# A decoder trunk on one core: hand-set spacing of the scan's chunks, earlier sums for the gated norm, and a new order of the projected rows

## The chip, the cores and the metric

The kernel runs on one core of a Trainium2 chip. It uses that core's matrix engine (PE, with its weight loads shown as PEld), the vector engine (DVE), the scalar engine (ACT), GpSimd (POOL) and the sync engine (SP), which here only issues transfers. The metric is the device time of one execution in microseconds. Three runs of the kernel before gave 2872.22, 2872.91 and 2874.28 us; their median is 2872.91 us. The profile is a separate execution.

## The reference, cut to what matters

The program is a two-layer trunk over 1040 tokens (16 learned ones and 1024 given) of width 1024. Layer one is a Mamba-2 style mixer and a gated convolutional feed-forward part, layer two is stick-breaking attention and another feed-forward part. The change touches only the mixer and the first lines behind it. Cut to its core, the mixer computes:

```python
z, xbc, dt_raw = jnp.split(u @ w_in, [2048, 2048 + 3072], axis=-1)
xbc = silu(causal_conv4(xbc, conv_w, conv_b))
xs, b_in, c_in = jnp.split(xbc, [2048, 2048 + 512], axis=-1)
# per group g of 4 (8 heads of 64 channels each), chunk by chunk:
y_diag = einsum('bgcls,bgecls,bcsgep->bclgep', cb, decay_in, xdt)
y = y_diag + y_off(state) + xs * d_skip
hg = (y * silu(z)).reshape(b, L, 4, 512)
hg = hg * rsqrt(mean(hg * hg, axis=-1) + eps) * gate_g
out = hg @ w_out
```

The chunk length is free, since any split of the scan gives the same sum; the kernel uses nine chunks of 116 tokens.

## The kernel before, in words

All matrices are float32 split into a high and a low part, so each product is three matmuls (`mm3`, L164 to L166). Rows of the program are 128 channels by 1040 tokens. A row is made in three **projection tiles** of 348, 348 and 344 tokens; one tile is 24 matmuls into one PSUM bank. Tiles of token block 2 go to the bank `ex`, those of blocks 0 and 1 to the two banks `mm`.

There are two kinds of projection tile. An **in-tile** makes a third of a row of x, b or c: after the matmuls, ACT writes the first tap of the convolution (L288), DVE adds three taps (L292), and ACT applies silu when the next tile settles (L480). A **gate tile** makes a third of a row of z: ACT takes silu out of PSUM (L512), DVE multiplies it onto the scanned row (`product`, L519), and with the next tile ACT squares the product (L524) and DVE adds it to the sum of squares (L528, L530).

`mixer` first loads and transposes the tokens with tiles from a pool named `start`, makes the six rows of group 0 in an order that the planner sets (`stream(into(0))`), and then enters a part whose order on PE, DVE, ACT and POOL is that of the program text (`manual_schedule`). SP is not in that list, and instructions of later parts may still be placed in between by the planner. In this part the scan of the four groups runs, nine chunks each. Around each chunk stand `ssd_front` (the products of b and c, transposes, weighting by the decays) and `ssd_back` (the new state, the outputs, the skip). Between the two, the program pulls projection tiles from the generator `work = stream(blocks)`. I number these tiles from 0 to 101: into(1) is 0 to 17, gate(0) 18 to 29, into(2) 30 to 47, gate(1) 48 to 59, into(3) 60 to 77, gate(2) 78 to 89, gate(3) 90 to 101. Two of them come before the first chunk. The chunks of groups 0 and 3 then take about two each, those of groups 1 and 2 take 4, 3, 3, 4, 3, 3, 4, 3, 3, and the last six come behind the last chunk. With the first of a chunk's tiles the loads of the next chunk's decays (`ssd_decays`, tiles D and E) are issued, with the second ACT computes them (L614, L615), with the third DVE multiplies c onto them (L618).

When a group's gate tiles are done, `gate_norm` normalises each token block: a matmul with ones sums the squares over partitions (L542), ACT copies that out of PSUM (L543), loads a function table (L188), takes logarithm and exponential (L546, L547), and DVE refines the root in four steps (`refine`, L551 to L553). Before, these calls are keyed so that block j runs ahead of tile n = 31 + j, 61 + j and 91 + j. For groups 0 and 1 the refinement and then four `spill` steps are queued in `self.spread`, of which one is taken after each tile; a spill scales one x row in three instructions (L557) and POOL stores it to memory (L706). For group 2 refinement and scaling follow at once, but for block 2 the scaling, which is spread. Group 2's rows stay in place, and `out_proj` splits them into high and low parts (`split`, L174 and L175) outside the ordered part. Group 3's norm is done by `end`.

All long rows come from one pool of 28 buffers (`Q`): 16 hold the normalised input u, six a group's rows. A row of group g + 2 can be written only when a buffer of group g is free, thus after its store has ended. Decays, states and the chunk's other tiles come from a pool named `ssd`, opened after `start` has been closed.

```python
calls[3 * len(todo) + 1 + j] = lambda f=f, j=j: f(j)
for _ in range((tiles * (c + 1) + 8) // 9 - given):
self.spread += [lambda q=q: spill(q) for q in range(4)]
dk = pool.tile([P, 1024], F32, tag="D", name=self.nm("D"))
```

Of the kernel before, what the change touches and what calls it, by code (L numbers as in the profile page):

```python
# [8 lines left out]
F32 = mybir.dt.float32  # L9
# [4 lines left out]
P = 128  # L14
D = 1024
# [28 lines left out]
DT0 = 0  # L44
LAG = 2
EARLY = 2

NW = 8
SUMS = ((6, 1), (3, 6), (7, 6), (3, 5), (5, 7)), ((4, 7), (2, 1))
# [19 lines left out]
class Trunk:  # L69
# [411 lines left out]

        return self.a["w_in"][col // P], tile

    def in_group(self, u, g, out):


        def block(col, cv):
# [13 lines left out]

    def gate_group(self, u, g, x, acc, later):

# [29 lines left out]

        return [block(q) for q in range(4)]

    def gate_norm(self, g, x, acc, j, table=True):
        s0, n = TT[j]
        nc, width = self.nc, DI // GROUPS
        tt = nc.vector.tensor_tensor
        v, r = acc.pop(j)[:, :n], self.tmp("y")[:, :n]  # L540
        ps = (self.mm if j else self.ex)("ms")[:, :n]
        nc.tensor.matmul(ps, self.ones, v, start=True, stop=True)  # L542
        nc.scalar.activation(v, ps, AF.Copy)  # L543
        if table:
            self.ln_exp()
        nc.scalar.activation(r, v, AF.Ln, scale=1.0 / width)  # L546
        nc.scalar.activation(r, r, AF.Exp, scale=-0.5)  # L547

        def refine():
            for _ in range(2):  # L550
                tt(v, v, r, op=ALU.mult)  # L551
            nc.vector.tensor_scalar(v, v, -0.5 / width, 1.5, op0=ALU.mult, op1=ALU.add)
            tt(r, r, v, op=ALU.mult)  # L553

        def scale(q):
            xq = x[q][:, s0 : s0 + n]
            nc.vector.scalar_tensor_tensor(xq, xq, self.par("gate_norm", 4 * g + q), r, op0=ALU.mult, op1=ALU.mult)  # L557

        return refine, scale

    def settle(self):

# [4 lines left out]
    def stream(self, blocks, w0=None):  # L567


        calls = {}  # L570
        todo = []
        for src, f in blocks:
            if src is None:
                for j in range(3):
                    calls[3 * len(todo) + 1 + j] = lambda f=f, j=j: f(j)
            else:
                todo.append((src, f))
        w = [w0 or self.load_w(todo[0][0], D)]
        for n in range(3 * len(todo)):
            i, j = divmod(n, 3)  # L580
            if j == 0:
                if i + 1 < len(todo):
                    w.append(self.load_w(todo[i + 1][0], D))
                cur = w.pop(0)
            if n in calls:
                calls.pop(n)()
            todo[i][1](cur, j)
            if self.spread:
                self.spread.pop(0)()
            yield  # L590
        self.settle()
        for f in chain(self.spread, calls.values()):
            f()

    def ssd_decays(self, g, ct, c, pool):

        nc = self.nc
        h0 = GH * g
        t0, n = CH[c]
        cc = 3 * (c % 3) + c // 3  # L600
        dk = pool.tile([P, 1024], F32, tag="D", name=self.nm("D"))
        dk = dk[:n, : GH * CB].rearrange("p (h l) -> p h l", h=GH)
        nc.sync.dma_start(dk, self.acs_d[c, h0 : h0 + GH].unsqueeze(0).to_broadcast([n, GH, CB]))
        dk = dk[:, :, :n]
        ce = None
        if c:
            ce = pool.tile([P, GH * CB], F32, tag="E", name=self.nm("E"), bufs=2)
            ce = ce.rearrange("p (h l) -> p h l", h=GH)
            nc.sync.dma_start(ce, self.ea_d[c, h0 : h0 + GH].unsqueeze(0).to_broadcast([P, GH, CB]))
            ce = ce[:, :, :n]  # L610
        yield dk, ce

        for i in range(GH):
            nc.scalar.activation(dk[:, i], dk[:, i], AF.Relu, scale=-1.0, bias=self.cols[:n, 1, cc, h0 + i : h0 + i + 1])  # L614
        nc.scalar.activation(dk, dk, AF.Exp, scale=-1.0)  # L615
        yield
        if c:
            nc.vector.tensor_tensor(ce, ce, ct[:, t0 : t0 + n].unsqueeze(1).to_broadcast([P, GH, n]), op=ALU.mult)  # L618
        yield
# [60 lines left out]
    def mixer(self, mx):  # L680
# [4 lines left out]
            dt = self.dt_path(*dt, mx)  # L685
        with self.tc.tile_pool(name="ssd", bufs=3) as pool:
            nc = self.nc
            yd, rows = [None] * 4, [[] for _ in range(4)]
            accs = [{} for _ in range(4)]
            done, waiting = [], []  # L690

# [4 lines left out]
                    waiting.append((j, f))  # L696

            def gate(g):
                scales = []

                def spill(q):
                    if q == 0:
                        yd[g] = self.dp.tile([4, P, L], F32, tag=f"y{g}_d", name=f"y{g}_d")
                    for f in scales:
                        f(q)
                    nc.gpsimd.dma_start(yd[g][q], rows[g][q][:, :L])  # L706

                def norm(j):
                    refine, scale = self.gate_norm(g, rows[g], accs[g], j)
# [17 lines left out]
            into = lambda g: self.in_group(u, g, rows[g])  # L727
# [8 lines left out]
            with self.tc.manual_schedule(engines={E.PE, E.DVE, E.Activation, E.Pool}):  # L736
# [3 lines left out]
                    next(work)  # L740
                for g in range(GROUPS):
                    *x, bt, ct = rows[g]
                    tiles, given = (18 - EARLY, 30, 30, 18)[g], 0
                    state = None
                    for c in range(9):
                        for _ in ahead:
                            pass
                        ops = self.ssd_front(g, x, bt, ct, c, dk, pool)
                        now = dk, ce
                        for _ in range((tiles * (c + 1) + 8) // 9 - given):  # L750
                            next(work)
                            if given == (tiles * c + 8) // 9:
                                nxt = (g, ct, c + 1) if c < 8 else (g + 1, rows[g + 1][5], 0) if g < 3 else None
                                ahead = self.ssd_decays(*nxt, pool) if nxt else iter([(None, None)])
                                dk, ce = next(ahead)
                            else:
                                next(ahead, None)
                            given += 1
                        state = self.ssd_back(g, x, c, *now, *ops, state, pool)
                        if g == 3:  # L760
                            done.append(c)
                            todo, waiting[:] = waiting[:], []
                            for w in todo:
                                later(*w)
                for _ in work:
                    pass

        def end():
            for j in range(3):
                refine, scale = self.gate_norm(3, rows[3], accs[3], j, j == 0)  # L770
                refine()
                for q in range(4):
                    scale(q)

        return hd, [r[:4] for r in rows], yd, end

    def out_proj(self, hd, ys, yd, end, pool):

        a = self.a
        h = [None] * KD  # L780
        banks = cycle((self.mm, self.lg, self.ex, self.mm, self.lg))
        for i, g in enumerate((2, 0, 1)):
            ops = [self.split(ys[g][q] if yd[g] is None else self.fetch(yd[g][q], "y"), "y") for q in range(4)]
            for f in range(KD):
                w = self.load_w(a["w_out_f"][g, f], 4 * P)
                if i == 0:
# [7 lines left out]
        ops = [[self.split_half(ys[3][q][:, L // 2 * x : L // 2 * (x + 1)], "y") for q in range(4)] for x in range(2)]  # L794
# [814 lines left out]
    def run(self, ctx):  # L1609
        tc = self.tc  # L1610
        with self.banks() as self.lp:
            with tc.tile_pool(name="mx", bufs=1) as mx:
                hd, ys, yd, end = self.mixer(mx)
            self.rp = ctx.enter_context(tc.tile_pool(name="rp", bufs=1))
            with tc.tile_pool(name="ff0", bufs=2) as pool:
                d, *forms = self.out_proj(hd, ys, yd, end, pool)
# [79 lines left out]
```

## Time and profile before

| what | value |
|---|---|
| median of three runs | 2872.91 us |
| profiled execution, time | 2871.28 us |
| profiled execution, span | 2869.6 us |
| mean granted PE clock | 0.995 |
| PE, DVE, ACT, POOL busy | 98%, 70%, 54%, 22% |
| chain that ended last | PE 81%, DVE 6%, ACT 4% |
| loading, transposing and rows of group 0 | about 0 to 123 us |
| scan with projection tiles 0 to 101 | 123.5 to 658 us |

Times in the views are microseconds from the start of the span. A group of instructions is named by its source line, its engine, its operation and its output and input tiles. Busy PE time counts pipelined matmuls from issue to a modelled end, so a matmul of 0.32 us may follow the one before it after 0.16 us.

### The profile page before, as it was taken

The page shows a single profiled execution, that of the slowest core. Times are in us where ns is not written, and L with a number is a line of the kernel's source. Part 1 is how long each engine was busy: PE and PEld are TensorE (multiplying, and loading weights), DVE is VectorE, ACT ScalarE, POOL GpSimd, SP SyncE. Part 2 cuts the span into 40 slices and gives each one's busy share as a digit, 9 for nine tenths or more (in the row PEclk, how much of TensorE's full clock was granted, in tenths as well). Part 3 has the DMA queues.
Part 4 walks back from the last instruction along what each step waited for, and adds up shares of the span by engine and source line. Part 5 has one row for each costly group of instructions (what it writes and reads, how often), then busy time and mean ns, then how long its engine had stood idle before and what let it go on. Part 6 is the DMA issues. An engine that isn't in the chain of part 4 may idle for free.

```text
span 2869.6 us, 54962 instructions
## 1 busy us (share of the span) xinstructions
PE 2815.9 (98%) x21808; PEld 2705.5 (94%) x21808; DVE 2003.3 (70%) x3736; ACT 1559.2 (54%) x3067; POOL 619.1 (22%) x542
## 2 busy tenths in 40 slices
PE   8999999999999999999999999999998999999998
PEld 5999898989999999999999999999998999999888
DVE  5685858776578656558886666666679565657895
ACT  5576767773245555556334555555636555555442
POOL 0000000000004666660000111101102666661000
PEclk9999999999999999999999999999999999999999
DMA  6233333324221222226232222222441222225331
GB/s 170 75 111 93 118 87 114 105 60 160 84 98 64 78 79 78 80 84 208 67 132 87 62 68 67 63 69 57 143 148 54 82 80 78 80 82 184 110 110 60
DMA packets 134128, 274.69 MB, mean 96 GB/s; under 512 B 16464, under 2 KB 68304, under 8 KB 133872
## 3 DMA queue, kind: packets, MB, share of 16 engines
q1 hardware_dynamic: 128560, 260.26, 28.4%
q10 hardware_dynamic: 4048, 6.36, 0.6%
q0 software_dynamic: 1264, 4.57, 0.4%
q8 instruction: 171, 2.80, 0.4%
q14 instruction: 85, 0.70, 0.1%
HBM read 203.02 MB, written 53.21 MB: 89 GB/s over the span
## 4 chain that ended last, share of the span: by engine, by line
PE 81%; DVE 6%; ACT 4%; issue 1%; DMA 0%; ACTq 0%; DVEq 0%; SPq 0%
PE p L166 10%; PE p L165 10%; PE p L164 10%; PE acc L166 8%; PE acc L165 8%; PE acc L164 8%; PE pj L164 5%; PE pj L165 5%; PE pj L166 5%; PE lg L1400 3%; PE po L1437 3%; PE wT L1422 3%; ACT D L614 1%; DVE xbc L292 1%; DVE bl L917 1%
## 5 line engine op out<-in xcount | busy, mean ns | idle before, releaser
L164 PE MATMUL pj<-uh,wh 128*128 128x348 f32 (+2 forms) x1536 | 502.2, 327 | 7.2 <-DVE xbc L292 6.1
L165 PE MATMUL pj<-ul,wh 128*128 128x348 f32 (+2 forms) x1536 | 495.6, 323 | 0.0
L166 PE MATMUL pj<-uh,wl 128*128 128x348 f32 (+2 forms) x1536 | 492.4, 321 | 0.0
L164 PE MATMUL p<-bh,fh 128*128 128x262 f32 (+1 forms) x1408 | 400.2, 285 | 9.0 <-DVE p L1041 5.2
L165 PE MATMUL p<-bl,fh 128*128 128x262 f32 (+1 forms) x1408 | 401.1, 285 | 0.4
L166 PE MATMUL p<-bh,fl 128*128 128x262 f32 (+1 forms) x1408 | 400.0, 284 | 0.0
L165 PE MATMUL p<-bl,wh 128*128 128x262 f32 (+1 forms) x1056 | 301.5, 286 | 1.9 <-DVE bl L917 1.9
L164 PE MATMUL p<-bh,wh 128*128 128x262 f32 (+1 forms) x1056 | 301.8, 286 | 1.5 <-ACT bh L916 1.0
L166 PE MATMUL p<-bh,wl 128*128 128x262 f32 (+1 forms) x1056 | 302.5, 286 | 0.0
L164 PEld LDWEIGHTS pj<-uh,wh 128*128 128x128 f32 x1536 | 289.2, 188 | 10.4 <-issue 7.7
L165 PEld LDWEIGHTS pj<-ul,wh 128*128 128x128 f32 x1536 | 289.6, 189 | 1.8 <-issue 0.6
L166 PEld LDWEIGHTS pj<-uh,wl 128*128 128x128 f32 x1536 | 289.1, 188 | 0.0
L164 PEld LDWEIGHTS p<-bh,fh 128*128 128x128 f32 x1408 | 268.1, 191 | 10.3 <-DVE p L1041 5.6
L292 DVE SCALAR_TENSOR_TENSOR c<-p,params,c 128x260 f32<-128x260 f32 (+1 forms) x440 | 207.8, 481 | 90.9 <-ACT c L288 89.0
L165 PEld LDWEIGHTS p<-bl,fh 128*128 128x128 f32 x1408 | 267.3, 190 | 1.4 <-DVE bl L917 1.2
L166 PEld LDWEIGHTS p<-bh,fl 128*128 128x128 f32 x1408 | 267.4, 190 | 0.2
L972 POOL TENSOR_TENSOR fl<-x,fh 128x1024 fp32r<-128x1024 f32 x80 | 192.5, 2406 | 256.0 <-ACT fh L971 255.9
L1041 DVE TENSOR_TENSOR p<-p,ft 128x262 f32<-128x262 f32 (+1 forms) x176 | 76.5, 436 | 214.2 <-ACT ft L1038 125.2
L165 PE MATMUL acc<-gl,wh 128*128 128x260 f32 (+1 forms) x672 | 211.1, 319 | 0.6 <-DVE gl L1139 0.5
L166 PE MATMUL acc<-gh,wl 128*128 128x260 f32 (+1 forms) x672 | 208.3, 319 | 0.0
L165 PEld LDWEIGHTS p<-bl,wh 128*128 128x128 f32 x1056 | 202.3, 192 | 2.5 <-DVE bl L917 2.3
L164 PEld LDWEIGHTS p<-bh,wh 128*128 128x128 f32 x1056 | 202.1, 191 | 2.1 <-ACT bh L916 1.2
(313 smaller groups left out, 7240.1 us busy)
## 6 DMA issues: line engine op xcount, KB each, us to landing
w<-in_w_up SPq DMA_DIRECT2D x92, 512.0 KB
w<-in_w_down SPq DMA_DIRECT2D x44, 512.0 KB
w<-in_w_in SPq DMA_DIRECT2D x40, 512.0 KB
E<-ea_d SPq DMA_DIRECT2D x32, 464.0 KB
D<-acs_d SPq DMA_DIRECT2D x32, 420.5 KB
g<-c SPq DMA_DIRECT2D x88, 130.0 KB
g<-c SPq DMA_DIRECT2D x88, 128.0 KB
b<-g SPq DMA_DIRECT2D x16, 520.0 KB
```

Source lines behind the costliest of these rows:

```text
L164: mm(out, wh, uh, start=first, stop=False, skip_group_check=joins)
L165: mm(out, wh, ul, start=False, stop=False, skip_group_check=joins)
L166: mm(out, wl, uh, start=False, stop=last, skip_group_check=joins)
L292: nc.vector.scalar_tensor_tensor(to, ps[:, o + i : o + i + n], wcol(i), out, op0=ALU.mult, op1=ALU.add)
L614: nc.scalar.activation(dk[:, i], dk[:, i], AF.Relu, scale=-1.0, bias=self.cols[:n, 1, cc, h0 + i : h0 + i + 1])
L917: tt(hl[1], x, hl[0].bitcast(F32), op=ALU.subtract)
L972: (self.nc.vector if b < 2 else self.nc.gpsimd).tensor_tensor(lo[:, :n], t, hi[:, :n].bitcast(F32), op=ALU.subtract)
L1041: add = lambda o, x, y: tt(o[:, :N], x[:, :N], y[:, :N], op=ALU.add)
L1400: nc.tensor.matmul(ps[:nt, a, :m], part[:, c0 : c0 + nt], ks[a][:, s0 : s0 + m], start=x == 0, stop=x == 1)
L1422: nc.tensor.transpose(pt[:ns, x * CB : x * CB + nt], kp[a][:nt, x * CB : x * CB + ns], self.ident[:nt, :nt])
L1437: nc.tensor.matmul(po[64 * a : 64 * a + 64, w], v[: CH[c][1], c, 64 * a : 64 * a + 64], wt[a][: CH[c][1], c, :nt], start=x == 0, stop=x == ...
```

## The change

It has five parts.

- **Spacing.** The number of tiles in each chunk is written out in `PACE`. Group 0 keeps its numbers. Groups 1 and 2 take 2 in each of the first six chunks (these are the gate tiles) and then 8, 5 and 5 (the in-tiles). Group 3 takes 2 in six chunks and 3 in the last three, so that three tiles are left behind the last chunk. The next chunk's decays are begun with the third tile from the end of a chunk, or with its first tile where it has fewer than three.
- **Sums a tile sooner.** The calls of `gate_norm` are keyed to 3 * len(todo) + j: ahead of tiles 30, 60 and 90 and their two followers. The PSUM bank is `ex` for block 1 and `mm` for blocks 0 and 2.
- **Roots in one go.** `gate_norm` now ends with the copy; logarithm and exponential are a function `root`. For groups 0 and 1 one entry of `spread` runs all three roots with one table load, then three refinements follow, then the four spills with an empty entry between each two. For group 2 root, refinement and scaling are as before.
- **Rows b and c first.** `in_group` makes b, c and then the four x rows. The b row of groups 0 and 2 comes from a buffer of its own in the pool `ssd`; D is 928 instead of 1024 wide.
- **The splits of group 2** are written into the ordered part: one row after each of the last three tiles, the fourth at the end.

```diff
+PACE = (2, 2, 2, 2, 1, 2, 2, 2, 1), (2, 2, 2, 2, 2, 2, 8, 5, 5), (2, 2, 2, 2, 2, 2, 8, 5, 5), (2, 2, 2, 2, 2, 2, 3, 3, 3)
...
-                    row.append(self.Q("xbc"))
-                    out.append(row[0])
+                    out[i] = pool.tile([P, L], F32, tag="row", name=self.nm("row"), bufs=1) if i == 4 and g % 2 == 0 else self.Q("xbc")
+                    row.append(out[i])
...
-        return [block(DI + (4 * g + q) * P, 4 * g + q) for q in range(4)] + [
-            block(2 * DI + g * P, 16 + g), block(2 * DI + (GROUPS + g) * P, 20 + g)]
+        return [block(2 * DI + g * P, 16 + g, 4), block(2 * DI + (GROUPS + g) * P, 20 + g, 5)] + [
+            block(DI + (4 * g + q) * P, 4 * g + q, q) for q in range(4)]
...
-        ps = (self.mm if j else self.ex)("ms")[:, :n]
+        ps = (self.ex if j == 1 else self.mm)("ms")[:, :n]
...
+        def root(table=True):
+            nonlocal r
+            r = self.tmp("y")[:, :n]
+            if table:
+                self.ln_exp()
+            nc.scalar.activation(r, v, AF.Ln, scale=1.0 / width)
+            nc.scalar.activation(r, r, AF.Exp, scale=-0.5)
...
-                    calls[3 * len(todo) + 1 + j] = lambda f=f, j=j: f(j)
+                    calls[3 * len(todo) + j] = lambda f=f, j=j: f(j)
...
-        dk = pool.tile([P, 1024], F32, tag="D", name=self.nm("D"))
+        dk = pool.tile([P, GH * CB], F32, tag="D", name=self.nm("D"))
...
+                def roots():
+                    for j in range(3):
+                        steps[j][0](j == 0)
...
-                        self.spread.append(refine)
-                        scales.append(scale)
                         if j == 2:
-                            self.spread += [lambda q=q: spill(q) for q in range(4)]
+                            wait, store = lambda: None, [lambda q=q: spill(q) for q in range(4)]
+                            self.spread += [roots, *(x[1] for x in steps), store[0], wait, store[1], wait, store[2], wait, store[3]]
                     else:
+                        root()
                         refine()
...
-                        for _ in range((tiles * (c + 1) + 8) // 9 - given):
+                        for i in range(PACE[g][c]):
                             next(work)
-                            if given == (tiles * c + 8) // 9:
+                            if i == max(0, PACE[g][c] - 3):
...
+                ops = []
                 for _ in work:
-                    pass
+                    ops.append(self.split(rows[2][len(ops)], "y"))
+                ops.append(self.split(rows[2][3], "y"))
```

More of the change, by code (lines that the diff above doesn't have):

```diff
@@ L482, in in_block, with in_group, block @@
         return self.a["w_in"][col // P], tile
-    def in_group(self, u, g, out):
-        def block(col, cv):
+    def in_group(self, u, g, out, pool):
+        def block(col, cv, i):
             row = []
@@ L534, in gate_group, with gate_norm @@
         return [block(q) for q in range(4)]
-    def gate_norm(self, g, x, acc, j, table=True):
+    def gate_norm(self, g, x, acc, j):
         s0, n = TT[j]
@@ L539, in gate_norm @@
         tt = nc.vector.tensor_tensor
-        v, r = acc.pop(j)[:, :n], self.tmp("y")[:, :n]
-        ps = (self.mm if j else self.ex)("ms")[:, :n]
+        v = acc.pop(j)[:, :n]
+        ps = (self.ex if j == 1 else self.mm)("ms")[:, :n]
         nc.tensor.matmul(ps, self.ones, v, start=True, stop=True)
         nc.scalar.activation(v, ps, AF.Copy)
[L544 to L547, printed above, removed]
+        r = None
+        def root(table=True):
[5 more added lines that the diff above has]
+            nc.scalar.activation(r, r, AF.Exp, scale=-0.5)
         def refine():
@@ L557, in scale @@
             nc.vector.scalar_tensor_tensor(xq, xq, self.par("gate_norm", 4 * g + q), r, op0=ALU.mult, op1=ALU.mult)
-        return refine, scale
+        return root, refine, scale
     def settle(self):
@@ L587, in stream @@
             todo[i][1](cur, j)
-            if self.spread:
-                self.spread.pop(0)()
+            for f in self.spread[:1]:
+                f()
+            del self.spread[:1]
             yield
@@ L687, in mixer @@
             nc = self.nc
-            yd, rows = [None] * 4, [[] for _ in range(4)]
+            yd, rows = [None] * 4, [[None] * 6 for _ in range(4)]
             accs = [{} for _ in range(4)]
@@ L703, in spill @@
                         yd[g] = self.dp.tile([4, P, L], F32, tag=f"y{g}_d", name=f"y{g}_d")
-                    for f in scales:
+                    for _, _, f in steps:
                         f(q)
@@ L725, in gate @@
                 return tiles + [(None, norm)] if g < 3 else tiles
-            into = lambda g: self.in_group(u, g, rows[g])
+            into = lambda g: self.in_group(u, g, rows[g], pool)
             blocks = into(1) + gate(0) + into(2) + gate(1) + into(3) + gate(2) + gate(3)
@@ L742, in mixer @@
                     *x, bt, ct = rows[g]
-                    tiles, given = (18 - EARLY, 30, 30, 18)[g], 0
                     state = None
@@ L764, in mixer @@
                                 later(*w)
+                ops = []
                 for _ in work:
-                    pass
+                    ops.append(self.split(rows[2][len(ops)], "y"))
+                ops.append(self.split(rows[2][3], "y"))
         def end():
             for j in range(3):
-                refine, scale = self.gate_norm(3, rows[3], accs[3], j, j == 0)
+                root, refine, scale = self.gate_norm(3, rows[3], accs[3], j)
+                root(j == 0)
                 refine()
@@ L773, in end, with out_proj @@
                     scale(q)
-        return hd, [r[:4] for r in rows], yd, end
-    def out_proj(self, hd, ys, yd, end, pool):
+        return hd, rows[3][:4], yd, ops, end
+    def out_proj(self, hd, y3, yd, y2, end, pool):
         a = self.a
@@ L782, in out_proj @@
         for i, g in enumerate((2, 0, 1)):
-            ops = [self.split(ys[g][q] if yd[g] is None else self.fetch(yd[g][q], "y"), "y") for q in range(4)]
+            ops = [self.split(self.fetch(yd[g][q], "y"), "y") for q in range(4)] if i else y2
             for f in range(KD):
@@ L793, in out_proj @@
                     self.accumulate(h, f, HB + s0, n, lambda i, f: (w[0][:, i * P : i * P + P], w[1][:, i * P : i * P + P]), ops, HB, None if i else next(banks))
-        ops = [[self.split_half(ys[3][q][:, L // 2 * x : L // 2 * (x + 1)], "y") for q in range(4)] for x in range(2)]
+        ops = [[self.split_half(y3[q][:, L // 2 * x : L // 2 * (x + 1)], "y") for q in range(4)] for x in range(2)]
         ws = self.last_weights(a["w_out"][12:], pool)
@@ L1612, in run @@
             with tc.tile_pool(name="mx", bufs=1) as mx:
-                hd, ys, yd, end = self.mixer(mx)
+                hd, y3, yd, y2, end = self.mixer(mx)
             self.rp = ctx.enter_context(tc.tile_pool(name="rp", bufs=1))
             with tc.tile_pool(name="ff0", bufs=2) as pool:
-                d, *forms = self.out_proj(hd, ys, yd, end, pool)
+                d, *forms = self.out_proj(hd, y3, yd, y2, end, pool)
                 g = self.up(0, *forms, pool)
```

8 lines of the change are left out of this document (4 added, 4 removed).

## The prediction

> **What bounds the kernel now.** I read the page first, then PE's waits in the scan, then the stages around each wait.
>
> ```profile
> span 2869.6 us, 54962 instructions
> PE 2815.9 (98%) x21808; PEld 2705.5 (94%) x21808; DVE 2003.3 (70%) x3736; ACT 1559.2 (54%) x3067; POOL 619.1 (22%) x542
> PE 81%; DVE 6%; ACT 4%; issue 1%; DMA 0%; ACTq 0%; DVEq 0%; SPq 0%
> ```
>
> PE sets the time and the change takes no matmul away, so it can only gain where PE stands still. PE's waits from 140 to 660 us (us in total, times, longest):
>
> ```profile
> PE y L672 <- issue: 6.5, 1, 6.5
> PE pj L164 <- DVE xbc L292: 5.6, 2, 2.8
> ```
>
> Two stalls of 2.8 us wait for a bank that DVE empties late. One of 6.5 us is marked "issue"; what it waited for is found below. Stages (length, busy time of PE, PEld, DVE, ACT and POOL, granted clock, DMA share, GB/s): the scan's undisturbed part, the stretch around the first stall, then each stall and what follows it.
>
> ```profile
> 526.60:593.40 66.80, 66.80 (x527) 61.32 (x526) 48.15 (x91) 51.36 (x104) 0.00 (x0) 1.00 0.37 107
> 285.00:340.00 55.00, 52.13 (x372) 48.31 (x371) 48.35 (x89) 41.78 (x74) 2.21 (x4) 0.99 0.35 117
> 339.10:343.00 3.90, 3.90 (x15) 3.90 (x16) 2.64 (x4) 3.88 (x10) 0.00 (x0) 0.59 0.44 135
> 490.70:494.60 3.90, 3.90 (x24) 3.90 (x25) 2.62 (x4) 3.88 (x10) 0.00 (x0) 1.00 0.40 131
> 625.00:631.60 6.60, 0.09 (x1) 0.03 (x1) 6.60 (x15) 3.66 (x7) 2.16 (x1) 0.80 0.00 1
> 631.60:636.00 4.40, 4.39 (x36) 4.12 (x37) 4.20 (x12) 2.96 (x6) 0.81 (x1) 0.52 0.00 0
> ```
>
> After the first stall the clock is 0.59 for 3.9 us: 0.41 x 3.9 = 1.6 us more. After the second, of the same length, it stays 1.00. After the third it is 0.52 for 4.4 us: 2.1 us more. So the prizes are **A** = 2.8 + 1.6 = 4.4, **B** = 2.8 and **C** = 6.5 + 2.1 = 8.6, together 15.8 us.
>
> [...]
>
> **The change, part by part.**
>
> *Spacing, roots and spread of groups 1 and 2 (A and B).* DVE's queue around the first stall, one store and one wait beside it:
>
> ```profile
> 302.24 1.79 DVE L292 SCALAR_TENSOR_TENSOR xbc<-pj,params,xbc 128x344 f32<-128x344 f32 x3
> 303.95 1.07 DVE L551 TENSOR_TENSOR z<-z,y 128x348 f32<-128x348 f32 x2
> ...
> 305.86 1.22 DVE L158 TENSOR_TENSOR wl<-w,wh 128x1024 fp32r<-128x1024 f32 x1
> 307.00 1.80 DVE L292 SCALAR_TENSOR_TENSOR xbc<-pj,params,xbc 128x348 f32<-128x348 f32 x3
> ...
> 329.87 1.55 DVE L557 SCALAR_TENSOR_TENSOR xbc<-xbc,params,y 128x348 f32<-128x348 f32 x3
> 331.33 1.12 DVE L618 TENSOR_TENSOR E<-E,xbc 128x928 f32<-128x928 f32 x1
> ...
> 337.17 1.79 DVE L292 SCALAR_TENSOR_TENSOR xbc<-pj,params,xbc 128x344 f32<-128x344 f32 x3
> ```
> ```profile
> 315.19 0.60 POOL L706 DMA_DIRECT2D y_d<-xbc  x1 [227.14 <-DVE xbc L557]
> ```
> ```profile
> 318.48 0.64 ACT L288 ACTIVATE xbc<-pj,params 128x348 f32<-128x348 f32 x1 [2.98 <-DMA y_d<-xbc]
> ```
>
> From start to start: a tile's taps 1.71, a refinement 1.91, the low half of a row's weights 1.14 (0.38 a tile), a spill 1.46, a chunk's own DVE work 5.84 us. A chunk with three in-tiles and three spills asks DVE for 5.84 + 3 x 2.09 + 3 x 1.46 = 16.5 us. PE needs less:
>
> ```profile
> 100.00:125.00 25.00, 25.00 (x158) 24.95 (x157) 12.82 (x22) 11.28 (x19) 0.00 (x0) 1.00 0.50 142
> ```
>
> 158 matmuls in 25 us make a tile of 24 about 3.8 us; the undisturbed stage has six chunks and 12 tiles, so a chunk costs PE (66.8 - 12 x 3.8)/6 = 3.5 us. Three tiles and a chunk are 14.9 us: DVE falls behind, and the taps of a tile queue behind a whole chunk (331.33 to 337.17).
>
> After, the first six chunks have two gate tiles each, which is what group 3's first six have in the undisturbed stage, where PE waits for nothing. The last three hold everything else: DVE 3 x 5.84 + 18 x 2.09 + 3 x 1.91 + 4 x 1.46 = 66.7 us against PE's 18 x 3.8 + 3 x 3.5 = 78.9. By prefix: the eight-tile chunk 29.8 against 33.9, the first of five 20.7 (three spills) against 22.5. DVE stays under PE at each step, with the two `mm` banks as reserve. ACT's roots become one block of a load and six activations, about 1.3 + 6 x 0.5 = 4.3 us, ahead of one tile's first tap; the tile behind it is then 1.5 us late in PSUM, less than a tile. Stores: the first spill now follows tile 36 and its buffer is written in tile 39, 11 us later, where the trace had the store's issue at 315.19 and ACT waiting on it to 318.48. So A and B go: +7.2. The bounds: 0, if DVE still lags, and 7.2.
>
> *Rows b and c first; b in its own buffer.* In the scan this only frees a buffer. At the start it costs. The b row's buffer lies in the pool that reuses the memory of the token tiles; if that memory is handed over as a whole, the first row's taps wait for the last token transpose.
>
> ```profile
> 42.87 0.63 ACT L288 ACTIVATE xbc<-pj,params 128x348 f32<-128x348 f32 x1
> ...
> 59.18 0.64 ACT L288 ACTIVATE xbc<-pj,params 128x348 f32<-128x348 f32 x1 [0.52 <-PE pj L166]
> ```
> ```profile
> 65.68 1.07 PE L329 MATMUL xT<-ident,x 128*128 128x128 f32 x6
> ...
> 131.19 0.36 PE L630 MATMUL cb<-xbc,xbc 128*116 128x116 f32 x2
> ```
> ```profile
> 26.00:66.70 40.70, 22.38 (x104) 16.19 (x104) 5.08 (x9) 1.92 (x3) 1.00 0.67 158
> ```
>
> Before, three tiles were already drained by 60 us, and 104 projection matmuls (the last row counts those alone) were done when the last transpose ended at 66.7. With three banks and none drained, 72 can be: 32 x 0.158 = 5.1 us of PE work is put off. Against that, transposes no longer compete with the 24 matmuls run just before 65.68 us, so they end up to 3.8 us sooner and draining begins sooner. Bounds 0 (the memory is handed over tile by tile) and 5.1, and 2.4 more if PE then waits for the first drain (0.64 + 3 taps). I take **3**, below the middle of 0 and 7.5 for the earlier transposes.
>
> *Group 3's last chunks (C), and the sums a tile sooner.* ACT, DVE and PE before:
>
> ```profile
> 595.52 1.05 ACT L157 ACTIVATE wh<-w 128x1024 fp32r<-128x1024 f32 x1
> ...
> 598.62 0.45 ACT L543 ACTIVATE z<-ms 128x348 f32<-128x348 f32 x1
> 599.10 1.28 ACT L188 ACT_TABLE_LOAD   x1
> ...
> 600.92 0.49 ACT L547 ACTIVATE y<-y 128x348 f32<-128x348 f32 x1
> ...
> 602.73 0.46 ACT L512 ACTIVATE z<-pj 128x348 f32<-128x348 f32 x1
> ...
> 618.79 2.33 ACT L614 ACTIVATE D<-D,cols 112x112 f32<-112x112 f32 x8
> ...
> 622.82 0.95 ACT L615 ACTIVATE D<-D 112x896 f32<-112x896 f32 x1
> ```
> ```profile
> 601.45 1.08 DVE L551 TENSOR_TENSOR z<-z,y 128x348 f32<-128x348 f32 x2 [1.72 <-ACT y L547]
> ...
> 605.46 0.52 DVE L519 TENSOR_TENSOR xbc<-xbc,z 128x348 f32<-128x348 f32 x1
> ...
> 621.54 0.52 DVE L175 TENSOR_TENSOR yl<-xbc,yh 128x348 fp32r<-128x348 f32 x1 [3.87 <-ACT yh L174]
> ...
> 630.42 1.08 DVE L639 TENSOR_TENSOR D<-D,cbm 112x896 f32<-112x896 f32 x1
> ```
> ```profile
> 593.40 0.41 PE L164 MATMUL pj<-uh,wh 128*128 128x348 f32 x1
> ...
> 597.27 0.75 PE L542 MATMUL ms<-z,ones 128*128 128x348 f32 x2
> ...
> 631.61 0.65 PE L672 MATMUL y<-D,xdt 112*64 112x112 f32 x4 [6.52 <-issue]
> ```
>
> The 6.5 us stall ends just after DVE has multiplied the last chunk's decays (630.42 + 1.08): that is what PE waited for. A norm holds ACT 4.1 us (598.62 to 602.73, two table loads in it), and the decays run behind three of them; DVE stood 3.87 us at a split that the planner had put there. After, the splits come behind the last chunk, and chunks 6 to 8 have three tiles. ACT's load in chunk 6 is three norms (12.3), decays with two loads (2.33 + 0.95 + 2 x 1.3 = 5.9) and three tiles (silu, a square as long, a third of the weights' 1.05, each overlapping the one before by 0.1: 3.4): 21.6 us in PE's 14.9 + 0.9 for the sums; in chunks 7 and 8 9.3 in 14.9. It is 5.8 us behind after chunk 6 and nearly level after chunk 7. Followed queue by queue, the last decays are ready about 1 us ahead of PE, chunk 7's operands 0.4 us. So C goes, with little room: if late, up to 5 us come back.
>
> **D**, a new wait: the first norm's refinement and scaling now stand on DVE ahead of the last squares' sum of block 2, and the third sum needs that. The chain from copy to refinement is 601.45 - 598.62 = 2.8 us and can begin at 596.6, when ACT has done the weights; refinement and scaling take 605.46 - 601.45 = 4.0, the sum 0.4: 603.8. PE, from 593.4 with two sums (0.3 each) and two tiles, is there at 601.6. Cost 2.2 us, bounds 0 (ACT earlier by the weights and a table load) and 5 (one more tile late); behind it on PE stand tile 92 and all the rest. The norms of groups 0 and 1 do not have it, since their refinements are spread.
>
> **E**, the last two splits need buffers of u and stand on ACT and DVE behind the last tile's silu: 3 copies and 3 subtractions of 0.5 us per row, pipelined, some 3 us until the fourth row's first third is there; PE has meanwhile six thirds of two rows to multiply (18 x 0.16 = 2.8) if they are taken in that order, half a microsecond in the program's. Bounds 0 and 3, I take **1**.
>
> Sum: 4.4 + 2.8 + 8.6 - 3 - 2.2 - 1 = **9.6 us** less than the profiled 2871.28, thus 2861.7; that execution lies 1.6 us under the median of the runs, against which it makes 2863.3. What a measurement of this kernel can tell from no change is about 0.2%, 5.7 us.
>
> **The rivals.**
>
> - *Nothing new waits.* 15.8 us come, 2857. For it: all new waits have 0 as a lower bound. Against it: the third sum's chain is read off from rows. Chance 0.15.
> - *The late taps stay.* The last three chunks now hold all in-tiles, the refinements and the spills, and a burst (weights, refinement, chunk) makes DVE late by more than the banks cover: A and B do not come, 9.6 - 7.2 = 2.4, 2870.5. For it: DVE is busy 48.35 of 55 us there. Against it: 66.7 against 78.9. Chance 0.12.
> - *The last decays are late again.* The spacing doesn't do what it is there for: chunk 7's 0.4 us are used up by instructions that the planner puts in. C does not come: 9.6 - 8.6 = 1, 2871.9. Chance 0.10.
> - *Slower: the start.* The first row's taps stand until 66.7 us, the transposes don't get faster, and only two banks fill (the third is the one in which the tokens' step sizes are summed): 104 - 48 = 56 matmuls, 8.8 us, then 2.4 us until a bank is drained and 3.2 us by the clock, twice the 1.6 measured above. 14.4 us against 15.8 - 3.2: 2874.7, slower from 12.6 us on. For it: the b row is the first in the new order, so its tiles fill both banks first. Against it: the planner can put transposes first. Chance 0.15, half of it beyond 2878.7.
>
> **How the numbers follow.** The forecast has 0.48, with its own range 2859 to 2867. Faster than 2867.2 are nearly all of it and the first rival: 0.60. Slower than 2878.7 is half of the last rival and a little for what the planner may shift elsewhere: 0.12. The rest is 0.28. The range goes from 2855, the first rival, to 2876, past the late decays and the slow start's own 2874.7.
>
> **What would show it.** A and B: no wait of `pj` for L292 between 280 and 520 us, and clock 1.00 there. C: no "issue" wait at the last L672. D: a wait of the third L542 of group 2 near 2 us. E: a gap ahead of the first `acc`. Start: the first L288 stands behind the last L329, and the first chunk (L630) begins later than 131.2 us. The prediction is wrong if PE's waits in the scan sum to as much as before, or if the first chunk is late by more than 8 us.

## The result and the profile after

The changed kernel takes 2852.80 us (median of 6 runs, 2852.52 to 2853.45) against 2872.88 us before (6 runs, 2872.22 to 2875.32): a ratio of 0.9929 with a 95% interval of 0.9917 to 0.9941, 20.1 us less. The forecast was 2863 with a range of 2855 to 2876, so the direction was right and the gain was twice the one I had worked out. The profiled executions are 2871.28 and 2852.52 us, 18.8 us apart; the sums below are made between these two.

The page of the kernel after (span, busy engines, chain):

```profile
span 2850.8 us, 54962 instructions
PE 2808.9 (99%) x21808; PEld 2698.9 (95%) x21808; DVE 2000.2 (70%) x3736; ACT 1551.8 (54%) x3060; POOL 619.2 (22%) x542
PE 87%; DVE 3%; DMA 1%; ACT 1%; issue 0%; ACTq 0%; DVEq 0%; SPq 0%
```

PE runs the same 21808 matmuls. ACT has 7 instructions fewer, which are table loads. The shares of DVE and ACT in the chain fell to 3% and 1%. PE's waits from 140 to 650 us of the kernel after (us in total, times, longest):

```profile
PE ms L543 <- DVE z L531: 1.5, 1, 1.5
PE S L667 <- DVE xde L654: 1.1, 1, 1.1
PE y L679 <- DVE D L646: 0.4, 1, 0.4
```

The two waits for taps and the "issue" wait are gone; the one new wait is the third sum of group 2's norm. The waits of 1.1 and 0.4 us were there before, with the same lengths. The same 535 us of both kernels, first before, then after, in the columns of the stages shown above:

```profile
125.00:660.00 535.00, 521.19 (x3871) 487.14 (x3870) 397.64 (x738) 380.95 (x725) 9.77 (x17) 0.99 0.32 96
```
```profile
125.00:660.00 535.00, 531.98 (x3961) 498.35 (x3960) 404.61 (x749) 377.63 (x730) 9.89 (x17) 1.00 0.35 105
```

PE has 90 matmuls more in them, at a clock of 1.00 against 0.99. Where the 18.8 us come from, by the first matmul of each part on PE (lengths in us; the first column is the time at which the first chunk begins):

| kernel | first chunk | group 0 | group 1 | group 2 | group 3 to first product of the output projection | output projection | first feed-forward part | rest |
|---|---|---|---|---|---|---|---|---|
| before | 131.2 | 93.8 | 151.5 | 150.1 | 131.4 | 192.8 | 711.8 | 1306.9 |
| after | 130.1 | 93.8 | 146.7 | 146.7 | 124.6 | 192.7 | 709.7 | 1306.5 |
| gain | 1.1 | 0 | 4.8 | 3.4 | 6.8 | 0.1 | 2.1 | 0.4 |

**The start.** ACT and PE of the kernel after around the last token transpose, the first chunk, and the projection matmuls alone up to 66.7 us:

```profile
59.54 0.49 ACT L272 ACTIVATE uh<-xT,params 128x272 fp32r<-128x272 f32 x1 [0.57 <-PE xT L330]
59.92 1.17 ACT L289 ACTIVATE row<-pj,params 128x348 f32<-128x348 f32 x2
```
```profile
58.96 0.54 PE L330 MATMUL xT<-ident,x 128*128 128x128 f32 x3
...
130.07 0.36 PE L637 MATMUL cb<-xbc,row 128*116 128x116 f32 x2
```
```profile
26.00:66.70 40.70, 21.71 (x93) 14.60 (x94) 3.72 (x7) 1.79 (x3) 1.00 0.70 159
```

The first taps of the b row (tile `row`, two at once) stand right behind the last transpose, where I had put them. But that transpose comes at 59.0 us and not at 65.7, and by 66.7 us PE has done 93 projection matmuls against 104. By 75 us it has done 145 against 143. All engines from 50 to 75 us, before and after:

```profile
50.00:75.00 25.00, 25.00 (x155) 22.08 (x154) 12.67 (x26) 12.01 (x23) 0.00 (x0) 1.00 0.39 124
```
```profile
50.00:75.00 25.00, 25.00 (x155) 22.23 (x156) 16.83 (x33) 15.27 (x26) 0.00 (x0) 1.00 0.42 135
```

PE is busy for all 25 us in both, with 155 matmuls each: 11 projection matmuls were put off, transposes and small products were done in their place, and by 75 us the 11 were made up.

**Groups 1 and 2.** The chunks with 8, 5 and 5 tiles of both groups, and group 3's last three with the last tiles, after:

```profile
290.60:368.80 78.20, 78.20 (x521) 75.57 (x519) 62.15 (x112) 47.86 (x87) 2.21 (x4) 1.00 0.32 103
442.00:515.00 73.00, 73.00 (x491) 70.84 (x490) 57.44 (x103) 43.76 (x81) 2.13 (x4) 1.00 0.33 98
583.00:642.00 59.00, 57.48 (x420) 54.26 (x417) 44.52 (x90) 40.81 (x77) 5.54 (x9) 1.00 0.15 47
```

DVE is busy 62.2 of 78.2 us in the packed chunks and PE never stands. In the last stretch PE misses 1.5 us of 59, the new wait:

```profile
594.40 0.85 PE L543 MATMUL ms<-z,ones 128*128 128x344 f32 x2 [1.52 <-DVE z L531]
...
641.71 0.32 PE L167 MATMUL pj<-uh,wl 128*128 128x344 f32 x1
641.86 0.32 PE L165 MATMUL acc<-yh,wh 128*128 128x348 f32 x1
```

The last two rows are the change from the last projection tile to the output projection: they are 0.15 us apart, so there is no gap for the late splits.

### The profile page after: what moved, and what is told of

Read it like the earlier page. It is cut to its first block, busy times and chain, and to the rows that moved or that the text cites. A ratio compares the mean times of both kernels' runs of the same rounds, so it can differ in the third digit from the quotient of the medians.

```text
span 2850.8 us, 54962 instructions
## 1 busy us (share of the span) xinstructions
PE 2808.9 (99%) x21808; PEld 2698.9 (95%) x21808; DVE 2000.2 (70%) x3736; ACT 1551.8 (54%) x3060; POOL 619.2 (22%) x542
## 4 chain that ended last, share of the span: by engine, by line
PE 87%; DVE 3%; DMA 1%; ACT 1%; issue 0%; ACTq 0%; DVEq 0%; SPq 0%
PE p L165 10%; PE p L167 10%; PE p L166 10%; PE acc L166 8%; PE acc L167 8%; PE acc L165 8%; PE pj L165 7%; PE pj L166 7%; PE pj L167 7%; PE lg L1413 3%; PE po L1450 3%; PE wT L1435 3%; PE y L679 1%; PE S L667 1%; PE y L681 1%; DVE bl L930 1%
## 5 line engine op out<-in xcount | busy, mean ns | idle before, releaser
L165 PE MATMUL acc<-gh,wh 128*128 128x260 f32 (+1 forms) x672 | 204.0, 319 | 0.0
```

The source lines that it names most:

```text
L165: mm(out, wh, uh, start=first, stop=False, skip_group_check=joins)
```

## The experiments

All times are medians beside the kernel before on the same chip; the stretches are those of the table above, from each run's trace. Kernel and trace of the changed kernel are the base unless said otherwise.

### The b row's buffer at the start

```diff
-... if i == 4 and g % 2 == 0 else self.Q("xbc")
+... if i == 4 and g == 2 else self.Q("xbc")
```

> The changed kernel, but only group 2's b row has the buffer of its own; group 0's b row comes from the common pool again, so its first taps need not wait for the token tiles' memory. Theory 1 (the wait is there, but PE fills it with transposes that then end sooner, so no PE time is lost): 2851.5 to 2854.5 us against 2852.8, the last transpose back from 59.3 to about 66 us, the first chunk within 1.5 us of 130.1. Theory 2 (the prediction's: the wait costs PE about 3 us): 2849 to 2850.5 us, the first chunk at about 127. Theory 3 (moving the transposes ahead was itself the gain of 1.1 us at the start): about 2854, the first chunk at 131.2.

Measured: 2856.57 us (2855.46 to 2857.12). The last transpose is back at 66.6 us and the first chunk at 131.3, as in theory 3; groups 1 to 3 keep 146.8, 146.8 and 124.7. So the wait is there and costs nothing; with it the first chunk comes 1.2 us sooner in this pair. That is no more than what the start varies by itself: in the kernels with the buffer it lies between 130.1 and 131.6 us though their instructions up to there stand in the same order, in those without it between 131.2 and 132.2. Of the 3.9 us between the two profiled executions, 1.2 lie here, 0.4 in the scan and the output projection and 2.5 in the first feed-forward part (712.2 against 709.7), which the edit does not touch; the rest is 0.2 shorter. So the time lies above the range of every theory.

### The old spacing in the changed kernel

```diff
-PACE = ..., (2, 2, 2, 2, 2, 2, 8, 5, 5), (2, 2, 2, 2, 2, 2, 8, 5, 5), (2, 2, 2, 2, 2, 2, 3, 3, 3)
+PACE = ..., (4, 3, 3, 4, 3, 3, 4, 3, 3), (4, 3, 3, 4, 3, 3, 4, 3, 3), (2, 2, 2, 2, 2, 2, 2, 2, 2)
-                            if i == max(0, PACE[g][c] - 3):
+                            if i == 0:
...
-                for _ in work:
-                    ops.append(self.split(rows[2][len(ops)], "y"))
+                for k, _ in enumerate(work):
+                    if k > 2:
+                        ops.append(self.split(rows[2][len(ops)], "y"))
```

> The changed kernel with the old spacing of the chunks: 4, 3, 3, 4, 3, 3, 4, 3, 3 tiles in groups 1 and 2, two in all of group 3, six tiles left at the end with the splits after the last three, decays begun with a chunk's first tile. Theory 1 (the spacing takes the stalls away): the waits of pj for DVE's taps come back in groups 1 and 2, 7 to 8 us, and some of the last chunk's stall, in all 2860 to 2867 us. Theory 2 (roots in one go, the empty entries between the spills and the new row order do it): groups 1 and 2 stay as in the changed kernel, within 1.5 us, in all 2852 to 2855 us.

Measured: 2868.98 us (2865.92 to 2870.31). Groups 1 and 2 take 155.1 and 153.5 us, which is 8.4 and 6.8 more than after, and 3.6 and 3.4 more than even before, and the time lies above theory 1's range: without the spacing, the rest of the change makes these groups longer. Which of its parts does so was not separated. PE's waits from 20 to 660 us of this kernel:

```profile
PE ms L543 <- DVE z L531: 4.0, 2, 2.0
PE S L667 <- DVE xde L654: 3.7, 5, 1.1
PE pj L165 <- DVE xbc L293: 3.6, 2, 1.8
PE pj L165 <- ACT z L544: 1.6, 1, 1.6
```

The sums, called a tile sooner, now wait for squares that DVE adds late, and projection tiles wait for taps and for the copy of a sum. But group 3's stretch is 124.9 us as after: the end does not need three tiles a chunk once the splits are in their place.

### The spacing alone, in the kernel before

```diff
-                        for _ in range((tiles * (c + 1) + 8) // 9 - given):
+                        for i in range(PACE[g][c]):
                             next(work)
-                            if given == (tiles * c + 8) // 9:
+                            if i == max(0, PACE[g][c] - 3):
```

> The kernel before with the new spacing alone (PACE, decays begun with the third tile from a chunk's end); sums, roots, spills, row order, buffers and splits as before. Theory 1 (the spacing is what takes the stalls of groups 1 and 2 away, and three tiles a chunk at the end are enough against the last stall): groups 1 and 2 together 7 to 9 us shorter, the end 5 to 7 us shorter, 2857 to 2861 us. Theory 2 (packed in-tiles need the spread spills and one-go roots as well): in groups 1 and 2 waits of pj for DVE's taps or of ACT for a store remain, 3 us or more, 2862 to 2868 us.

Measured: 2861.16 us (2860.57 to 2862.26) against 2873.19. Groups 1 and 2 take 147.1 us each, so 7.4 of the 8.2 us come by the spacing alone; ACT waits there 6.3 us for two stores (5.0 in the changed kernel with its empty entries) and PE does not notice. From group 3 to the first feed-forward part it gains 3.1 us (321.1 against 324.2), where the changed kernel gains 6.9 (317.3): the last chunk's stall is halved and not gone. So theory 1 holds for groups 1 and 2 and not for the end. PE's waits from 125 to 660 us:

```profile
PE y L673 <- DVE D L640: 3.4, 2, 3.0
PE S L661 <- DVE xde L648: 1.1, 1, 1.1
PE pj L165 <- ACT z L544: 0.8, 1, 0.8
```

### The splits alone, in the kernel before

```diff
-                for _ in work:
-                    pass
+                self.y2 = []
+                for k, _ in enumerate(work):
+                    if k > 2:
+                        self.y2.append(self.split(rows[2][len(self.y2)], "y"))
+                self.y2.append(self.split(rows[2][3], "y"))
```

> The kernel before with only group 2's splits moved: into the ordered part, one row after each of the last three tiles, the fourth at the end. Theory 1 (the planner's splits ahead of the last decays are what makes the last stall of 6.5 us and its slow clock): the stretch from group 3's first chunk to the first product of the output projection falls from 131.4 to 123 to 126 us, 2865 to 2868 us in all. Theory 2 (ACT's three norms are the cause, and only more tiles per chunk cover them): that stretch stays above 129 us, 2870 to 2874 us.

Measured: 2862.12 us (2861.44 to 2863.02) against 2873.19. The stretch from group 3 is 123.3 us against 131.4: 8.1 of the 8.6 us of C, with two tiles a chunk and the norms as before. The whole gains more than theory 1 said, since the first feed-forward part takes 709.8 us against 711.8 here. PE's waits from 125 to 660 us:

```profile
PE pj L164 <- DVE xbc L292: 5.6, 2, 2.8
PE S L660 <- DVE xde L647: 1.1, 1, 1.1
PE y L672 <- DVE D L639: 0.8, 2, 0.4
```

The 6.5 us wait is gone, the two for taps are as before. So the splits that the planner had put ahead of the last decays made that stall; three norms on ACT alone do not.

### The splits left to the planner, in the changed kernel

```diff
                 for _ in work:
-                    ops.append(self.split(rows[2][len(ops)], "y"))
-                ops.append(self.split(rows[2][3], "y"))
+                    pass
+                ops = rows[2][:4]
```

The output projection then splits them.

> The changed kernel, but group 2's splits stand outside the ordered part again, where the planner places them. Theory 1 (the planner's splits ahead of the last decays made the 6.5 us stall): the last chunk's outputs wait again on DVE for 3 us or more, with a clock at half behind it, 2856 to 2862 us. Theory 2 (three tiles a chunk are cover enough): 2852 to 2854 us.

Measured: 2856.23 us (2855.39 to 2856.51). Group 3's stretch is 125.5 us, and up to the first feed-forward part 317.7 against 317.3: in the scan theory 2 holds. With everything else of the change the planner's splits cost 0.4 us. The 3.4 us by which it is slower are again behind: 712.7 us in the first feed-forward part against 709.7.

### The norm of group 2 spread

```diff
-                        root()
-                        refine()
-                        todo = [lambda q=q: [scale(q), scale(q + 1)] for q in (0, 2)]
-                        if j == 2:
-                            self.spread += todo
-                        else:
-                            for f in todo:
-                                f()
+                        self.spread += [lambda: [root(), refine()], *(lambda q=q: [scale(q), scale(q + 1)] for q in (0, 2))]
```

> The changed kernel, but group 2's roots, refinements and scalings are spread one entry a tile after the sums, so that nothing of them stands ahead of the third sum on ACT and DVE. Theory 1 (the third sum's wait of 1.5 us is the first norm's refinement and scaling ahead of the last squares' sum): that wait goes, tile 92 begins 1.5 us sooner, and the time is 2850.8 to 2851.8 us. Theory 2 (ACT and DVE are behind there by their whole load, and the wait only moves): 2852.3 to 2855 us with a new wait in the last three chunks.

Measured: 2853.28 us (2852.19 to 2853.62). The third sum's wait is gone and group 3's stretch falls from 124.6 to 122.8 us, as theory 1 has it; the whole time does not follow, since this run's start was 1.5 us later and its first feed-forward part 1.1 us longer. So the wait's cause is shown, and a gain over the changed kernel is not.

### Two tiles in every chunk of group 0

```diff
-EARLY = 2
-PACE = (2, 2, 2, 2, 1, 2, 2, 2, 1), ...
+EARLY = 0
+PACE = (2, 2, 2, 2, 2, 2, 2, 2, 2), ...
```

This stands on top of the spread norm.

> The changed kernel with group 2's norm spread as in the run late_refine, and no tile ahead of the first chunk: two tiles in every chunk of group 0, so that no chunk there has only one. Theory 1 (what is left of PE's waits in the scan, 1.1 us ahead of the state's product, 0.4 ahead of the outputs and 1.5 ahead of the third sum, is all short cover of a single wait each): the three go, group 0's stretch gets 1.5 us shorter, 2849.5 to 2851.5 us. Theory 2 (the two tiles ahead of the first chunk cover its decays' transfer and exponential): a wait of 2 us or more at the first chunk's outputs, 2852 to 2855 us.

Measured: 2857.05 us (2855.96 to 2857.35). The three short waits went, as expected, and a new one came: the first chunk now begins at 96.1 us, and PE waits for DVE's taps (17 to 660 us; below it, ACT and DVE ahead of the longest one):

```profile
PE pj L165 <- DVE xbc L293: 3.2, 2, 2.7
PE dtr L355 <- ACT h L347: 1.0, 1, 1.0
PE xT L330 <- ACT h L347: 0.5, 1, 0.5
```
```profile
101.58 2.37 ACT L621 ACTIVATE D<-D,cols 116x116 f32<-116x116 f32 x8 [6.24 <-DMA D<-acs_d]
...
104.91 1.81 DVE L293 SCALAR_TENSOR_TENSOR xbc<-pj,params,xbc 128x348 f32<-128x348 f32 x3 [8.11 <-ACT xbc L289]
```

The transfer of the first decays is issued at 93.6 us, right behind the stores of the step sizes that it reads; ACT stands 6.24 us for it, and the next tile's first tap stands behind the decays. This is the cause that theory 2 named, the transfer without tiles to cover it, but the wait shows at a projection tile and not at the first chunk's outputs, and the time lies above its range. Group 1 begins at 228.0 us against 223.9.

### The old roots and spills

```diff
+                        root()
+                        self.spread.append(refine)
                         if j == 2:
-                            wait, store = ...
-                            self.spread += [roots, *(x[1] for x in steps), store[0], wait, store[1], wait, store[2], wait, store[3]]
+                            self.spread += [lambda q=q: spill(q) for q in range(4)]
```

> The changed kernel, but the roots of groups 0 and 1 are taken at each norm with a table load each, refinements and spills follow without empty entries, as before. Theory 1 (with the new spacing DVE and ACT have room, and roots in one go and the empty entries bring nothing more): groups 1 and 2 within 0.5 us of 146.7 each, 2852 to 2854 us. Theory 2 (the packed tiles need them): a wait of pj for taps or of ACT for a store makes PE wait 2 us or more in each group, 2857 to 2860 us.

Measured: 2854.76 us (2854.02 to 2855.23). Groups 1 and 2 take 147.0 us each against 146.7, as theory 1 has it; the time is 0.8 us above its range. With the new spacing the one-go roots and empty entries are worth 0.3 us a group; the first feed-forward part is 1.2 us longer here.

### What differs behind the scan: both kernels again, and two changes of buffers

> The kernel before once more, unchanged, as a control of what differs from run to run behind the scan. If the pace of the first feed-forward part's matmuls (121.9 ns apart, against 121.4 in the changed kernel) and the two stretches of half clock at 868 and 878 us belong to the program, both come again; if to the execution, they change.

> The changed kernel once more, unchanged, as a control: if the pace of 121.4 ns and the absence of half-clock stretches between 850 and 900 us belong to the program, both come again; if to the execution, they change, and with them the 2.6 us that the trace gained behind the scan.

The kernel before again took 2876.52 us, the changed one 2853.11, one run each. The stretch of both traces with nothing but the first feed-forward part's matmuls (before, after; the second executions have 2462 and 2473 again):

```profile
938.00:1238.00 300.00, 300.00 (x2462) 300.00 (x2461) 179.02 (x385) 164.71 (x322) 201.01 (x119) 1.00 0.23 79
```
```profile
938.00:1238.00 300.00, 300.00 (x2473) 300.00 (x2473) 180.30 (x387) 166.86 (x327) 202.34 (x120) 1.00 0.24 78
```

The pace belongs to the program: 11 matmuls more in 300 us, 1.3 us, in both executions. The half clock at the entry of the part does not come again in the same way: the kernel before has it from 868 and from 878 us in one execution and from 884 us alone in the other, the changed kernel in neither.

The pace moves with edits that do not touch this part. In the same 300 us PE does 2462 matmuls in the run b_row_from_pool, 2464 in planner_splits, 2465 in old_roots and 2467 in spacing_alone, but 2473 or 2474 in splits_alone, old_spacing, late_refine and even_group0. The edit of the first of these only changes where one row's buffer comes from, so the buffers are a candidate. Two edits that could change which buffers hold the operands:

```diff
-            own = {i: (self.Q("bh", F32R), self.Q("bl", F32R)) for i in (0, 2, 3, 4, 6)}
+            own = {i: (self.Q("bl", F32R), self.Q("bh", F32R))[::-1] for i in (0, 2, 3, 4, 6)}
```

> The changed kernel, but in the feed-forward part's entry the low halves take their buffers from the common pool ahead of the high ones; the work is the same. Theory 1 (the pace of that part's matmuls, 121.4 ns in some kernels and 121.7 to 121.9 in others, follows which buffers hold the operands): the pace changes by 0.2 ns or more and the time by 0.7 us or more. Theory 2 (it follows something else): the pace stays at 121.43 and the time within 0.7 us of 2852.8.

```diff
+                if i == 1 and f == 0:
+                    self.nc.gpsimd.tensor_copy(self.Q("turn")[:, :HALO], self.zero)
```

> The changed kernel with one idle buffer of the common pool taken and given back on GpSimd during the output projection (a copy of four columns), so that the buffers that the feed-forward part takes afterwards can be other ones; no other work changes. Theory 1 (the pace of the first feed-forward part's matmuls follows which buffers hold the operands): the pace leaves 121.43 ns, by 0.2 ns or more, and the time changes by 0.7 us or more. Theory 2 (it does not): pace and time stay, 2852.3 to 2853.6 us.

Measured: 2853.61 and 2853.66 us, 2473 matmuls in that stretch in both: the pace did not move. The traces do not show which buffers were taken, so this does not rule buffers out; what sets the pace is open.

## Why the prediction was wrong in size

**What bounds the kernel, and the spacing (A and B): right.** Both stalls went, and the slow clock behind the first (0.59 for 3.9 us before, 1.00 from 125 to 660 us after), and the spacing alone does 7.4 us of it, as the working of DVE's demand had it. Sized 7.2, measured 8.2: A 4.8 for 4.4 and B 3.4 for 2.8. The price of B hung on one execution. In the second execution of the kernel before the same wait, from 489.11 to 491.93 us, did cost the clock:

```profile
487.81:491.22 3.41, 1.30 (x9) 1.01 (x7) 3.34 (x7) 0.00 (x0) 0.00 (x0) 1.00 0.01 2
491.22:494.64 3.42, 2.71 (x9) 2.74 (x10) 3.35 (x5) 2.80 (x10) 0.00 (x0) 0.50 0.21 29
494.64:498.05 3.41, 3.41 (x13) 3.41 (x13) 0.59 (x3) 3.38 (x4) 0.00 (x0) 0.50 0.32 125
```

Group 2 took 152.9 us there and not 150.1, 2.8 of the 5.2 us by which that execution was longer. This may be one reason why runs of the kernel before spread over 3 to 6 us and those of the changed one over 1, in whose scan no wait cost the clock in either execution (1.00 from 125 to 660 us in both). It may also be why the medians lie 1.3 us further apart than the profiled pair; neither was tested.

**Rows b and c first, own buffer: the step that failed.** Its mechanism was right, the first taps do wait for the last transpose. Its price, 3 us, came from counting the 32 projection matmuls put off as PE time lost, up to 5.1 us. Measured were 11 put off by 66.7 us and none by 75. The planner gave PE other work meanwhile: PE stayed at 25.00 of 25 us, and the transposes ended 7 us sooner. I had named the sooner transposes and taken only part of them. Measured 1.1 us gained instead of 3 lost: 4.1 us of the miss. That the term is near nothing is shown; the 1.1 us themselves are within what the start varies by from kernel to kernel.

**Group 3's end: right in kind, wrong in its share.** C, the splits ahead of the last decays, was named as what made DVE stand 3.87 us, and beside it ACT's three norms with the three tiles to cover them. In the kernel before, the splits alone are worth 8.1 us and the spacing without them 3.1; either covers in part for the other, so they do not add up. D was in its place and cost 1.5 us for 2.2; E, the late splits, cost nothing for 1: PE ran without a gap from 641.86 us, though the low halves of the last two rows were ready only from 644.7 to 647.3 us. The prediction had allowed for this, if PE takes the ready rows first. Sized 8.6 - 2.2 - 1 = 5.4, measured 6.8.

**Behind the scan: not in the sum.** 2.6 us, 2.1 of them in the first feed-forward part, which the change does not touch. 1.3 is the pace shown above. The rest, 0.8 us, goes with the clock at the entry of that part, where PE stands in both kernels alike. The stall there and the 3.4 to 4 us behind it, before and after:

```profile
863.00:868.00 5.00, 2.90 (x24) 2.69 (x23) 5.00 (x15) 1.93 (x4) 0.00 (x0) 1.00 0.00 0
868.00:871.40 3.40, 3.40 (x18) 3.40 (x17) 3.40 (x11) 2.67 (x9) 0.00 (x0) 0.50 0.03 7
```
```profile
847.00:852.00 5.00, 2.90 (x24) 2.69 (x23) 5.00 (x14) 1.78 (x3) 0.00 (x0) 1.00 0.00 0
852.00:856.00 4.00, 3.00 (x23) 2.59 (x22) 4.00 (x12) 3.33 (x10) 0.00 (x0) 1.00 0.02 4
```

The same idle time is followed by half clock in the one and by full clock in the other. No part of the change was aimed at either, so these 2.6 us are luck as far as the forecast goes.

In sum: 9.6 + 4.1 (start) + 1.0 (A and B) + 1.4 (end) + 2.6 (behind) = 18.7 us, of 18.8 measured. The rivals: "nothing new waits" came nearest with 15.8, but not as it was described, since the third sum did wait 1.5 us and 2.6 us came from behind the scan. "The late taps stay" and "the last decays are late again" did not occur. The slow start did not either, though the wait from which it was to come did. Nearly two thirds of the range lay above the forecast, for late decays and a slow start that did not come, and only 8 us below it; the forecast charged the new waits to PE before asking whether PE had something else to do.

## What to carry to other kernels

A wait that a change adds costs the bounding engine only if that engine has nothing else in reach: look whether it has idle time in that stretch, not whether some of its work is put off (here 11 projection matmuls were put off at the start while PE was busy for 25.00 of 25 us, and the first chunk came 1.1 us sooner). Work that a planner may place is best put behind the last chain that it can delay; here four splits written in their place were worth 8 us alone in the kernel before, and 0.4 us where the spacing already gave cover. Give a busy helper engine's bursts the longest stretches of the bounding engine: six short chunks and three long ones took away what even chunks could not (147.1 us for each of groups 1 and 2 against 151.5 and 150.1), while the rest of the change without that spacing made the same groups longer (155.1 and 153.5).

## What the runs showed of the hardware

The same PE stall does not always cost the same. A wait of 2.8 us was followed by a clock of 0.59 for 3.9 us (first stall) and by 1.00 (second) in one execution, by 0.57 for 3.8 and by 0.50 for 5.2 us in the next one: three of these four stalls of 2.8 us cost the clock. Pricing such a stall from one profile missed by 2.8 us here (group 2: 150.1 against 152.9 us).

In the scan, the traces show how these stalls differ. In the profiled execution of the kernel before, the stretches of half clock begin whole steps of 3.413 us apart (at 338.89, 629.02 and 867.96 us, the second 85 and the third 155 steps after the first), and they last one such step or two (3.41, 6.83 and 3.41 us). Cut at these steps, the first stall and the second (487.88 to 490.68 us) of that execution look so:

```profile
335.48:338.89 3.41, 0.84 (x6) 0.54 (x4) 3.34 (x7) 0.00 (x0) 0.00 (x0) 1.00 0.00 0
338.89:342.30 3.41, 3.20 (x11) 3.23 (x12) 2.85 (x5) 3.29 (x10) 0.00 (x0) 0.50 0.34 88
485.66:489.08 3.42, 2.22 (x14) 1.93 (x12) 3.42 (x9) 0.00 (x0) 0.00 (x0) 1.00 0.07 28
489.08:492.49 3.41, 1.81 (x11) 1.84 (x12) 3.30 (x6) 1.92 (x7) 0.00 (x0) 1.00 0.00 0
```

The first stall leaves PE idle for 2.6 us of one step, and the next step runs at half clock. The second is divided over two steps, with 1.2 and 1.6 us, and the clock stays at 1.00. In the second execution the steps fall otherwise: 2.1 us of the second stall lie in one of them, and the clock behind it is 0.50. From 125 us to the end of the scan of the first execution, the two steps at full clock with 2.6 and 3.4 us of idle PE (the second from 625.61 us) were followed by half clock, and none with 1.6 us or less was. The changed kernel's trace, cut from its first half clock at 2157.19 us, has no step there with more than 1.01 us, and its clock stays at 1.00. At the entry of a feed-forward part, where PE has short waits between short bursts, the idle time does not separate the cases: in the changed kernel 1.2 us of it, in the step from 2174.26 us at the entry of the second part, were followed by a clock of 0.50, while the 1.6 us from 489.08 us above were not.

The pace of one unchanged loop of matmuls differed by 0.5% between programs (2462 to 2474 in 300 us) and came again in each of them that was run twice. What sets it was not found.
